# An earlier opening, a feed-forward convolution tracked by halves, and paired output stores in an eight-core decoder-block kernel

## The chip, the cores and the metric

One Trainium2 chip (trn2), eight cores, one launch of one program on all of them. The metric is the device time of the slowest core, in microseconds (us). The eight cores sit on two dies (cores 0 to 3 and 4 to 7). In some executions the cores of one die or of both run at a lower granted TensorE clock and the time is some per cent longer; such runs are called slow here and are left out of every comparison. The engines are PE (matmul), PEld (its weight load), DVE (vector), ACT (scalar, with lookup tables), POOL (GpSimd) and SP (SyncE); POOL and SP issue the DMAs.

## The reference

A decoder block for a batch of 4 sequences of 2048 tokens with 2048 features, all float32:

```python
h = rmsnorm(x)
b, c, u, q, k, v, o, i, f = split(h @ w_in)
y_c = b * dwconv3_causal(c * u)                  # short gated convolution, 1024 channels
y_m = sigmoid(o) * rmsnorm_per_head(mlstm(q, k, v, i, f))   # 4 heads, a recurrence over the sequence
x = x + concat(y_c, y_m) @ w_out
g, u = split(dwconv3_causal(rmsnorm(x) @ w_up) + bias)      # 2 x 5632 channels
x = x + (silu(g) * u) @ w_down
x = x + sigmoid(rmsnorm(x) @ w_ple_gate) * (p @ w_ple_proj)
out = rmsnorm_final(x)
```

Each sequence is shared by two cores. The even core ("role 0") owns the first 1056 tokens, the odd core ("role 1") the last 992; because of the recurrence, role 1 also reads the tokens before its own, in slabs of 128, and computes their keys and gates.

## The kernel before

One program holds the instruction lists of both roles. Each engine reads its role from memory and branches:

```python
def both(e, eng):
    v = eng.value_load(role)
    with eng.If(v == 0):
        run(progs[0], e, eng)
    with eng.Else():
        run(progs[1], e, eng)
```

The lists come from Python code. `P.op` and `mm` append an instruction at once; `later(instruction, priority, waits)` puts it into a pool from which a scheduling model picks by modelled readiness and priority (0 first), `need(item)` forces it out, `flush_items()` empties the pool at the end. So the order on each engine is fixed at build time, and an engine executes its list in order: an instruction that waits holds up all that stand behind it.

The opening of role 1 (cuts marked `...`):

```python
P.op("sp", ... cst <- cst_p)                 # constants
if role:
    slab_load(0)
    slab_load(1)
P.op("sp", ... tct <- cst_t)                 # tables
P.op("pool", ... wif <- w_if)                # gate weights
P.op("pool", ... ident_bf <- cst_i)          # identity
...
def prefix_k(pump):                          # role 1
    k0, k1 = ip["k0"], ip["k1"]              # the first two key weights, 4 loads each
    slab_load(2, [k0.loads[2]])              # waits for a weight load
    pump()
    slab_load(3, [k1.loads[2]])
    ...
```

The feed-forward convolution. The up projection comes in units `c`; the first few handle one slice of the tokens at a time (there are two slices), the others both. Behind each unit stands this chain on ACT and DVE, and the units behind it need ACT for the copies that free PSUM:

```python
HW = NOWN // 2                               # where the two halves of the buffer are cut
RYv = [[RS("yv%d%d" % (j, h), Yo[j] + 4 * HW * h, 4 * HW) for h in range(2)] for j in range(2)]
...
def f():
    a = 0 if 0 in slices else 2 * QE - OFF   # where the two slices meet
    e_ = NOWN if 1 in slices else 2 * QE - OFF
    ...
    prev = cmult.get("last", [])             # the last product, of whatever slice
    yh = [h for h in range(2) if h * HW < e_ and h * HW + HW > a]
    for j in range(2):                       # gate half, value half
        it = later(s_act(yv, C(OFF), AF.Identity, ... bias, scale=w[2]), 1, ev + prev)    # ACT
        for t in (1, 0):
            it = later(s_stt(yv[:, z:], C(OFF - 2 + t + z)..., w[t], ...), 1, [it])       # DVE
        if j == 0:
            it = later(s_act(yv, yv, AF.Silu, Ry, Ry), 1, [it])                           # ACT
        fin.append(it)
    ...
    ms.append(later(s_tt(... ALU.mult ...), 1, fin))                                      # DVE product
    cmult["last"] = ms
```

The end: after the last gate unit of a slice, 16 normalisation products and 16 stores:

```python
def final(s):
    def f():
        nf.rs(s)
        for k in range(16):
            x, Rx = nf.xs(k, s)
            i = later(s_stt(x, x, cs(PC_GF + k), nf.acc[s], ...), 1, nf.rdy[s])
            later(("sp", ... outTv[:, k, 2*QO*s : 2*QO*(s+1)] <- x ...), 1, [i])
    return f
...
run_units(units, slots)
flush_items()
```

The softmax here doesn't subtract the row's maximum and nothing guards it: scores larger than these inputs give would overflow.

## Time and profile before

| | before |
|---|---|
| time, median of the first 5 runs | 1611.38 us (1611.2 to 1839.99, the highest a slow run) |
| span of the profiled run, even cores | 1596.9 to 1601.0 us |
| span of the profiled run, odd cores | 1605.0 to 1609.1 us |
| PE busy | 92% of the span |

A line of a timeline reads: start in us, busy us, engine, line of the program, operation, output<-input, count, and in brackets how long the engine had stood idle before and what released it. Nearly every instruction passes through a helper, so the line numbers mostly name the helper: in the kernel before, 328 is ACT, 333 and 337 are DVE, 352 is a matmul; in the changed kernel these are 334, 339, 343 and 358. Lines 348 (before) and 354 (changed) are transposes, lines from 1000 on DMAs and memsets of the opening. A line of a windows view gives the busy time of each engine in a stretch and, as its last three numbers, the granted clock, the DMA share and GB/s. An ACT_TABLE_LOAD marks a change of function on ACT; as every run has the same sequence of them, they serve as milestones.

### The profile page before, as it was taken

The page shows a single profiled execution, that of the slowest core. Times are in us where ns is not written, and L with a number is a line of the kernel's source. Part 1 is how long each engine was busy: PE and PEld are TensorE (multiplying, and loading weights), DVE is VectorE, ACT ScalarE, POOL GpSimd, SP SyncE. Part 2 cuts the span into 40 slices and gives each one's busy share as a digit, 9 for nine tenths or more (in the row PEclk, how much of TensorE's full clock was granted, in tenths as well). Part 3 has the DMA queues.
Part 4 walks back from the last instruction along what each step waited for, and adds up shares of the span by engine and source line. Part 5 has one row for each costly group of instructions (what it writes and reads, how often), then busy time and mean ns, then how long its engine had stood idle before and what let it go on. Part 6 is the DMA issues. An engine that isn't in the chain of part 4 may idle for free.

```text
span 1609.1 us, 36850 instructions; the slowest of 8 cores (1596.9 to 1609.1 us)
## 1 busy us (share of the span) xinstructions
PE 1485.8 (92%) x13634; PEld 1267.8 (79%) x13634; DVE 1169.8 (73%) x1802; ACT 592.8 (37%) x1054; POOL 248.4 (15%) x472
## 2 busy tenths in 40 slices
PE   2989999999998997999999999999999998998984
PEld 2865899898877885888888888888898886866763
DVE  2464333387768787888788877888778887879976
ACT  1652324577421123443034420444302444223453
POOL 1001111011112010111211122111121112211100
PEclk9989999999999998999999999999999999999997
DMA  6901644445758242464666556555566665745413
GB/s 166 318 31 26 101 85 74 96 62 123 152 81 149 35 73 47 67 92 61 84 107 91 78 71 104 91 89 80 79 89 98 91 88 86 99 68 85 78 66 138
DMA packets 80937, 148.82 MB, mean 92 GB/s; under 512 B 9072, under 2 KB 34288, under 8 KB 79728
## 3 DMA queue, kind: packets, MB, share of 16 engines
q0 software_dynamic: 67648, 112.90, 46.5%
q1 hardware_dynamic: 13104, 33.47, 6.0%
q8 instruction: 114, 1.87, 0.5%
q14 instruction: 71, 0.58, 0.1%
HBM read 251.08 MB, written 8.13 MB: 161 GB/s over the span
## 4 chain that ended last, share of the span: by engine, by line
PE 78%; DMA 8%; DVE 6%; issue 4%; ACT 2%; SPq 1%; POOL 1%; DVEq 0%; POOLq 0%; ACTq 0%
PE PS L352 77%; DVE M L333 3%; DMA M<-w_down_p 3%; DVE M L337 3%; ACT M L328 2%; DMA M<-xsl 1%; DMA M<-xr 1%; DMA M<-w_in_p 1%; DMA M<-pT 1%; PE PS L348 1%; DMA M<-w_up_p 1%; POOL M L588 0%; DMA M<-w_pg_p 0%; ACT L328 0%; SPq L1018 0%
## 5 line engine op out<-in xcount | busy, mean ns | idle before, releaser
L352 PE MATMUL PS<-M 128*128 128x250 bf16 (+6 forms) x13330 | 1473.3, 270 | 105.1 <-ACT M L328 42.9
L352 PEld LDWEIGHTS PS<-M 128*128 128x128 bf16 (+1 forms) x13330 | 1249.7, 99 | 320.4 <-issue 166.2
L333 DVE TENSOR_TENSOR M<-M 128x992 bf16<-128x992 f32 (+18 forms) x716 | 494.9, 710 | 86.6 <-PE PS L352 40.7
L328 ACT ACTIVATE M<-PS 128x500 f32<-128x500 f32 (+8 forms) x490 | 238.2, 494 | 542.5 <-PE PS L352 532.8
L337 DVE SCALAR_TENSOR_TENSOR M<-M 128x992 f32<-128x992 f32 (+9 forms) x378 | 353.5, 981 | 54.3 <-ACT M L328 52.9
L328 ACT ACTIVATE M<-M 128x992 f32<-128x992 f32 (+10 forms) x398 | 308.6, 803 | 220.4 <-DVE M L333 154.9
L333 DVE TENSOR_TENSOR M<-M,PS 128x496 f32<-128x496 f32 (+6 forms) x443 | 251.1, 568 | 115.2 <-PE PS L352 110.7
L333 DVE TENSOR_TENSOR M<-PS,M 128x500 f32<-128x500 f32 (+13 forms) x191 | 102.0, 538 | 128.5 <-PE PS L352 115.4
L588 POOL DMA_DIRECT2D M<-w_up_p x176 | 93.1, 529 | 473.3 <-DVE M L333 228.8
L588 POOL DMA_DIRECT2D M<-w_in_p x96 | 50.9, 535 | 392.3 <-PE PS L352 211.7
L328 ACT ACTIVATE PS<-PS 128x500 f32<-128x500 f32 (+1 forms) x57 | 31.3, 549 | 214.1 <-PE PS L352 214.0
L588 POOL DMA_DIRECT2D M<-w_down_p x128 | 67.7, 529 | 229.1 <-PE PS L352 173.6
L328 ACT ACTIVATE M<-PS,M 126x256 bf16<-126x256 bf16 (+4 forms) x68 | 30.1, 483 | 15.5 <-DVE M L333 12.7
L588 POOL DMA_DIRECT2D M<-w_pg_p x32 | 16.9, 532 | 96.0 <-PE PS L352 89.7
L588 POOL DMA_DIRECT2D M<-w_out_p x32 | 16.9, 531 | 57.4 <-PE PS L352 52.3
L1156 DVE COPY M<-PS 128x1024 bf16<-128x1024 bf16 x9 | 6.2, 691 | 25.2 <-PE PS L348 25.2
L348 PE MATMUL PS<-M 128*128 128x128 bf16 (+4 forms) x304 | 22.6, 219 | 1.3 <-ACT M L328 0.9
L348 PEld LDWEIGHTS PS<-M 128*128 128x128 bf16 (+4 forms) x304 | 19.9, 110 | 3.1 <-issue 2.6
L328 ACT ACT_TABLE_LOAD x9 | 11.5, 1283 | 9.6 <-DVE M L1025 7.0
L337 DVE SCALAR_TENSOR_TENSOR M<-M,PS 128x256 f32<-128x256 f32 x24 | 10.7, 476 | 0.0
L1027 DVE CAST M<-M 128x128 bf16<-128x128 f32 x1 | 0.4, 365 | 13.6 <-DMA M<-cst_i 13.6
L328 ACT ACTIVATION_READ_ACCUMULATOR M<-PS 126x1 f32 (+1 forms) x32 | 6.4, 200 | 0.0
(22 smaller groups left out, 12.4 us busy)
## 6 DMA issues: line engine op xcount, KB each, us to landing
M<-w_up_p POOLq DMA_DIRECT2D x176, 256.0 KB, 4.8
M<-w_in_p POOLq DMA_DIRECT2D x96, 256.0 KB, 6.1
M<-w_down_p POOLq DMA_DIRECT2D x64, 192.0 KB, 4.2
M<-w_down_p POOLq DMA_DIRECT2D x64, 160.0 KB, 3.9
M<-xsl SPq DMA_DIRECT2D x8, 1024.0 KB, 10.6
M<-w_out_p POOLq DMA_DIRECT2D x32, 256.0 KB, 5.9
M<-w_pg_p POOLq DMA_DIRECT2D x32, 256.0 KB, 5.5
M<-xr SPq DMA_DIRECT2D x32, 250.0 KB, 7.6
```

Source lines behind the costliest of these rows:

```text
L328: return ("act", lambda e: e.activation(out=out, in_=in_, func=func, **kw), reads, writes, c)
L333: return ("dve", lambda e: e.tensor_tensor(out=out, in0=in0, in1=in1, op=op), reads, writes, c)
L337: return ("dve", lambda e: e.scalar_tensor_tensor(out=out, in0=in0, scalar=scalar, in1=in1, op0=op0, op1=op1), reads, writes, c)
L348: return ("pe", lambda e: e.transpose(out, in_, ident), reads, writes, 0.065)
L352: return ("pe", lambda e: e.matmul(out, lhsT=lhsT, rhs=rhs, start=start, stop=stop, skip_group_check=skip), reads, writes, c)
L588: p.loads.append(P.op("pool", lambda e, d=d, sr=sr: e.dma_start(out=d, in_=sr), [], [p.R[nm]], dma=True, cost=p.KT * 0.25, after=g))
L1027: P.op("dve", lambda e: e.tensor_copy(out=ones_bf, in_=onesF), [Rcst], [Rcbf])
L1156: it = later(("dve", lambda e, o=tr_out, i=tr_in: e.tensor_copy(out=o, in_=i), [RPS[7]], tr_R, 1.2), 0)
```

## The change

Its intent is to take idle time of PE out of three places: the opening (start the big loads before the role is known, and let the longer role fall through the branch), the first units of the up projection (let the convolution of one slice not wait for the other's product), and the end (fewer and larger stores, final products out of the way). A fourth part turns the ring of weight slots round, so that the first key weights have the same address in both roles. The core of the diff:

```diff
+COMMON = {"sp": 2, "pool": 5}
 ...
         def both(e, eng):
+            n = COMMON.get(e, 0)
+            run(progs[0], e, eng, 0, n)          # constants, xf; identity, 4 loads of k0
             v = eng.value_load(role)
-            with eng.If(v == 0):
-                run(progs[0], e, eng)
+            with eng.If(v == 1):
+                run(progs[1], e, eng, n)
             with eng.Else():
-                run(progs[1], e, eng)
+                run(progs[0], e, eng, n)
 ...
+    xf_op = P.op("sp", ... 1.08 MB block: slab 1 in role 1, feature tiles 0 to 3 in role 0)
 ...
     def prefix_k(pump):
         k0, k1 = ip["k0"], ip["k1"]
-        slab_load(2, [k0.loads[2]])
+        wif_load()
+        slab_load(2)
         pump()
         slab_load(3, [k1.loads[2]])
-        for c in range(4, NSB + 1):
+        for c in range(4, NSB + 2):
             slab_load(c)
 ...
-    ring = [Slot(GB + 2048 * i, 0, 10 ** 9) for i in range(NRING)]
+    ring = [Slot(CB - 2048 * (i + 1), 0, 10 ** 9) for i in range(NRING)]
+    ip["k0"].pin = dict(zip(RAWQ, ring))
 ...
-    HW = NOWN // 2
+    HW = 2 * QE - OFF
 ...
+    clast = [[], []]
 ...
-            prev = cmult.get("last", [])
-            yh = [h for h in range(2) if h * HW < e_ and h * HW + HW > a]
+            prev = [it for h in slices for it in clast[h]]
+            yh = slices
 ...
-            cread[c] = rd                        # the steps that read unit c's buffers
+            cread.setdefault(c, []).extend(rd)   # ... of both slices
 ...
-            cmult["last"] = ms
+            for h in slices:
+                clast[h] = ms
 ...
-                i = later(s_stt(x, x, cs(PC_GF + k), ...), 1, nf.rdy[s])
-                later(("sp", ... one tile ...), 1, [i])
+                its.append(later(s_stt(x, x, cs(PC_GF + k + j), ...), 2, nf.rdy[s]))
+            later(("sp", ... two tiles ...), 2, its)
 ...
     run_units(units, slots)
+    fill(10.0 ** 9, 0.0)                         # emit leftover work by modelled readiness
     flush_items()
```

Cut are the data preparation for `xf`, the new order and conditions of the other opening loads, a rewriting of the last stage's code for a mode that is not used (`if False`), and the memsets that moved earlier.

## The prediction

> **What bounds the kernel now.** I read the spans of all cores first. The program has two roles: even cores own 1056 tokens of a sequence (role 0), odd cores own 992 and in addition work through the prefix of their sequence (role 1). The time is that of the slowest core.
>
> ```profile
> core 0: 1596.9 us, clock 0.982
> core 1: 1609.1 us, clock 0.977
> core 4: 1601.0 us, clock 0.980
> core 5: 1605.0 us, clock 0.979
> ```
>
> The reader is to see that the odd cores set the time (1605.0 to 1609.1) and that the even ones follow 4 to 12 us behind (1596.9 to 1601.0). So a gain in role 1 counts only down to what role 0 then takes. PE is busy 92% on both, in steady stages 99 of 100 us; a change that leaves the matmuls alone can win only in the stages where PE idles. I looked for these with 100 us windows on cores 0 and 1: PE is busy 61 to 62 us in the first hundred, 86 to 87 in the one that holds the start of the up projection, 87 to 91 in 1300 to 1500, and idle in the last 17 to 20 us. These are the stages that the diff touches.
>
> The opening: SyncE's queue in the timeline of core 0, then core 1, then core 1's chain of waits.
>
> ```profile
> 2.51 0.39 SPq L1018 DMA_DIRECT2D M<-cst_p  x1
> 2.95 0.42 SPq L1022 DMA_DIRECT2D M<-cst_t  x1
> ...
> 6.52 4.60 SPq L1018 DMA_DIRECT2D M<-cst_p  x1
> 11.18 0.89 SPq L1011 DMA_DIRECT2D M<-xsl  x2
> ...
> 26.14 12.31 SPq L1011 DMA_DIRECT2D M<-xsl  x7
> ...
> 2.38 4.14 issue
> 6.52 4.60 SPq L1018
> 11.65 7.56 DMA M<-xsl
> 20.78 13.50 DMA M<-w_in_p
> 36.83 15.67 DMA M<-xsl
> ```
>
> Role 0 starts its first DMA at 2.51 us. Role 1, which sits in the Else half, starts it at 6.52 and the second one 4.6 us later. Nothing in the program lies between; both gaps are 4.0 and 4.2 us. Then slab 1, the first key weights and slab 2 arrive in turn, and PE does its first real matmul at 27.44 us and reaches the steady part at 37.7.
>
> The up projection (core 1, then core 0), the last up unit (core 1), and the end (core 1's last DVE group; core 0's windows, whose last three numbers are clock, DMA share and GB/s):
>
> ```profile
> 639.65 1.50 ACT L328 ACTIVATE M<-M 128x500 f32<-128x500 f32 x2 [2.61 <-DVE M L333]
> 641.77 3.49 PE L352 MATMUL PS<-M 128*128 128x250 bf16 x16 [8.25 <-ACT PS L328]
> ...
> 572.32 3.02 PE L352 MATMUL PS<-M 128*128 128x264 bf16 x13 [7.21 <-ACT PS L328]
> ...
> 1363.65 0.37 PE L352 MATMUL PS<-M 128*128 128x248 bf16 x1 [6.45 <-DVE M L333]
> ...
> 1594.93 10.43 DVE L337 SCALAR_TENSOR_TENSOR M<-M 128x496 f32<-128x496 f32 x16 [4.61 <-ACT M L328]
> ...
> 1591.00:1592.00 1.00, 0.00 (x0) 0.00 (x0) 0.00 (x0) 0.00 (x0) 0.00 (x0) 0.50 0.48 182
> 1596.00:1597.00 1.00, 0.00 (x0) 0.00 (x0) 0.00 (x0) 0.00 (x0) 0.00 (x0) 0.50 0.00 0
> ```
>
> PE waits 8.25 and 7.21 us for a PSUM copy on ACT, which stands behind a chain of convolution steps that alternate between ACT and DVE. At the end core 0's outputs have landed by 1592, yet its span goes on to 1596.9; core 1's DMA ends near 1607.4 and its span at 1609.1.
>
> **What the Trainium skill says.** "Runtime: NRT & Kernel Launch", section "Instruction fetch mechanics": prefetch is sequential, and a taken branch to a target outside the current two pages must fetch that page first. The trace agrees: role 1 jumps at the start (first DMA 4.0 us later than role 0), role 0 jumps over the other body at the end (about 4 us without data traffic). "DMA: Bandwidth & Descriptors", section "Anatomy of one DMA — SWDGE (gpsimd) path": about 2.0 us fixed plus bytes over 436 GB/s. The lone output DMAs of 248 KB landed in 2.1 us here, below that sum of 2.6; in the opening the engines are saturated (share 1.0) at 310 to 350 GB/s for plain loads, and I use these. "ScalarE: Activation LUTs", section "What ACT_TABLE_LOAD costs": 1283 ns; the trace has 1.28 us for each load, one of them inside the convolution chain.
>
> **The change, part by part.**
>
> Part 1, the opening. Constants, a 1.08 MB block "xf" (slab 1 in role 1; the first 4 of 16 feature tiles in role 0), the identity and the 4 first weight loads go ahead of the role's register load and branch; the branch is turned round, so role 1 falls through and role 0 jumps.
> Role 1: first DMA at about 1.0 instead of 6.5, slab 1 issued at about 1.4 instead of 11.6. Weights k0 (1 MB as bf16, 2 MB read) issued at about 2 to 4 instead of 13 to 15. Bytes read before k1 has landed: 0.3 constants, 1.1 slab 1, 2 k0, 0.1 and 0.2 tables, 0.2 slab 0, 1.05 slab 2 (it no longer waits for k0), 2 k1: 6.9 MB, at 310 GB/s 22 us, plus 2: the second weight pair is there at about 24 to 25. Before, the steady part began at 37.7, so 12 to 13 us are gained. After that PE has 9 to 10 of 10 us busy until 80, so it keeps the gain if the loads keep up: slabs 3 to 8 and the first half of its own tokens are 10.4 MB, at 330 GB/s 32 us from 23, so landed by 57; PE wants them from about 62. I take 12.
> Role 0: the jump moves to its front. SyncE would issue tile 4 at about 11 instead of 5.8. But by then 3.4 MB have been issued, which keep the DMA engines busy to about 13, so there is no hole; the other 12 tiles and gate weights (3.5 MB, 11 us) are in by about 25, as now (chain: last xr wait ends at 24.5). I take 0, plus or minus 3.
> At the end the jump changes sides as well: role 0 saves about 4 us (its 4.9 us after the outputs, less the 1.6 that core 1 needs, is 3.3 to 4), role 1 pays 4.
>
> Part 2, the convolution by halves. Sliced units used to wait for the previous product whatever its half, and in role 1 the halves of the buffer were cut at 496 although the slices meet at 492, so slice 1 really waited for both. Now each half has its own list and cut. DVE's idle gaps in that chain are 2.21 + 1.05 + 1.50 + 1.00 = 5.8 us on core 1 and 1.79 + 1.08 + 1.56 + 0.94 = 5.4 on core 0; two independent chains can fill most of them, but DVE has 14 us of convolution to do there in any case, and the kernel's own scheduling model decides the order. I take 4 us in role 1 and 3 in role 0. At the last up unit role 1 loses its wait on the product (1.04 us): 1.
>
> Part 3, the end. Outputs leave as 8 pairs of tiles instead of 16 tiles per slice, normalisation products have the lowest priority, and leftover work is emitted by modelled readiness. The last product group is 16 instructions by 0.65 us, 10.43 us, unchanged; its DMA is now twice as large, at most 0.6 us more. The first slice's products stand in DVE's way in the last 40 us (PE waits 0.5 to 1.7 us each, about 5 in all on core 1): 1 us gained net.
>
> Part 4, the ring of weight slots is turned round and k0 pinned in it; same number of slots. 0.
>
> Sums: role 1: 1609.1 - 12 - 4 - 1 - 1 + 4 = 1595; role 0: 1601.0 + 0 - 3 - 1 - 4 = 1593 at most, core 0 near 1589. The slowest is then a role 1 core at 1595, and the measured time stands 2.3 us above the span (1611.38 against 1609.1): **1597 us**, 0.9% less.
>
> **The rivals.** (a) The opening of role 1 is bound by total DMA traffic, not by its start: its engines are at share 1.0 from 15 to 80 us. Then the gain is the earlier start of real traffic, 12 to about 3, with some idle time given back: 8 to 9 instead of 12, and the time 1601. For it: the chain names xr loads until 74.6. Against: PE and ACT did not wait for them there. (b) Role 0 becomes the bound: its jump costs 4 us twice (first and second page, as role 1 shows) and a hole in DMA appears, so its first norm slips by 5 or more. Then core 4 stands at 1598 and the time at 1600 to 1602. For it: POOL in role 1 had its first DMA as late as 11.80. Against: the common block covers that time. (c) Part 2 works fully and the modelled order suits: 8 us instead of 4 in each role, and the time is 1592. (d) The new order of products and pairs costs at the end, where little overlaps: up to 3 us, 1600.
>
> **Range and chances.** The rivals lie from 1592 to 1602, and cores of one role differ by 4 us in one run: low 1589, high 1605. Over 2% faster would need less than 1579: all of PE's idle time in the opening and the up stage together; 4%. Slower by over 2% has no mechanism, except a new serial wait that I have not seen: 1%. Within 2%: 95%.
>
> **What would show it.** In the changed kernel: first DMA of every core near 1 us; role 1's slab 1 landed by 10, its steady key matmuls from about 25, and everything in it about 12 us earlier at 200 us; role 0 with its second group of DMAs near 6 to 11 us and its first norm still ending near 33; PE's 8.25 and 7.21 us waits in the up stage halved; about 4 us between last output and end on odd cores, under 2 on even ones. I am wrong if role 1 at 200 us is less than 8 us ahead, if even cores become the slowest by more than 3 us, or if the up stage keeps its waits.

## The result, and the profile after

| | before | changed |
|---|---|---|
| time, median | 1611.38 us (15 runs, 1608.39 to 1839.99) | 1587.15 us (8 runs, 1586.15 to 1588.92) |
| ratio of the fast runs | | 0.9851, 95% interval 0.9841 to 0.9861 |
| profiled run, even cores | 1596.9 to 1601.0 us | 1579.9 to 1582.1 us |
| profiled run, odd cores | 1605.0 to 1609.1 us | 1580.9 to 1583.5 us |

A ratio is the mean time of one kernel's fast runs over that of the other's fast runs of the same rounds, so it is not quite the ratio of the medians in the table. The change is worth 1.5%: within 2%, as predicted, but 24 us rather than 14, and 1587.15 us lies below the predicted range of 1589 to 1605.

The cores of the changed kernel:

```profile
core 0: 1580.3 us, clock 0.988
core 1: 1581.5 us, clock 0.981
core 3: 1583.5 us, clock 0.983
```

The two roles, 8 us apart before, now end nearly together. The milestones on one core of each role show where the time went (start of the instruction in us; the difference is how far ahead the changed kernel is, and a step between rows is what a stage gave):

| milestone | core 1 before | after | ahead | core 0 before | after | ahead |
|---|---|---|---|---|---|---|
| 2nd table load, opening is over | 192.00 | 178.77 | 13.2 | 110.27 | 115.18 | -4.9 |
| 3rd table load | 317.16 | 303.92 | 13.2 | 235.85 | 240.76 | -4.9 |
| silu table load, up projection starts | 630.22 | 617.13 | 13.1 | 563.18 | 565.27 | -2.1 |
| third PSUM copy of the full up units | 670.41 | 644.32 | 26.1 | 601.09 | 591.86 | 9.2 |
| table load at the end of the up stage | 1428.91 | 1402.42 | 26.5 | 1397.40 | 1390.00 | 7.4 |
| start of the last slice | 1559.30 | 1533.47 | 25.8 | 1541.32 | 1531.56 | 9.8 |
| last table load | 1592.24 | 1561.60 | 30.6 | 1575.36 | 1562.11 | 13.3 |
| end | 1609.1 | 1581.5 | 27.6 | 1596.9 | 1580.3 | 16.6 |

Three places give the time: the opening (role 1 only; role 0 loses there), the 40 us after the silu table load (13 and 11 us), and the last slice (4.8 and 3.5 us). The last row has the branch and the new stores at the end: role 1 gives back 3.0, role 0 gains 3.3. The other steps of core 0 (2.8 us before the silu table load, 2.4 us before the last slice) are stretches that vary by as much between cores; they come under what stays open.

The opening after, first core 1, then core 0, from their timelines:

```profile
1.07 0.39 SPq L1049 DMA_DIRECT2D M<-cst_p  x1
3.21 0.07 DVE L1060 MEMSET M<- 128x9 f32 x1 [3.21 <-issue]
7.51 0.33 SPq L1051 DMA_DIRECT2D M<-cst_t  x1
...
19.72 10.11 PE L358 MATMUL PS<-M 128*128 128x8 bf16 x136 [0.57 <-DMA M<-w_if]
...
29.67 0.61 PE L354 MATMUL PS<-M 128*128 128x128 bf16 x8
```

```profile
1.06 0.39 SPq L1049 DMA_DIRECT2D M<-cst_p  x1
10.92 0.06 DVE L1060 MEMSET M<- 128x1 f32 x1 [10.92 <-issue]
15.55 0.33 SPq L1051 DMA_DIRECT2D M<-cst_t  x1
```

and the line of before, core 1, that answers to the last one of the first fence:

```profile
43.48 0.61 PE L348 MATMUL PS<-M 128*128 128x128 bf16 x8
```

Both cores start their first DMA at 1.06 to 1.07 us. The transposes that come with the second key weights stand 13.8 us earlier on core 1. The jump is now role 0's: DVE, which has nothing to wait for, starts at 10.92 us where core 1's starts at 3.21, and SyncE resumes only at 15.55 us (12.9 to 15.6 on the four even cores), after what looks like a second stop, as role 1 had it before between 6.52 and 11.18 us.

The up projection of before, core 1, timeline (the two lines that stand after the second of these, at 639.65 and 641.77, are in the prediction):

```profile
630.22 1.28 ACT L328 ACT_TABLE_LOAD   x1
...
638.82 0.74 DVE L333 TENSOR_TENSOR M<-M 128x248 bf16<-128x248 f32 x2
...
641.06 0.57 ACT L328 ACTIVATE PS<-PS 128x500 f32<-128x500 f32 x1
```

and after, core 1:

```profile
607.46 0.79 ACT L334 ACTIVATE M<-M 128x500 f32<-128x500 f32 x1
...
609.19 0.79 ACT L334 ACTIVATE M<-M 128x500 f32<-128x500 f32 x1
...
617.13 1.28 ACT L334 ACT_TABLE_LOAD   x1
618.43 0.61 ACT L334 ACTIVATE M<-M 128x492 f32<-128x492 f32 x1
618.95 0.57 ACT L334 ACTIVATE PS<-PS 128x500 f32<-128x500 f32 x1
619.45 0.60 ACT L334 ACTIVATE M<-M 128x500 f32<-128x500 f32 x1
...
623.51 26.73 PE L358 MATMUL PS<-M 128*128 128x250 bf16 x246 [1.31 <-ACT M L334]
```

The copy that PE waits for is the ACTIVATE from PS to PS. Before, it starts 10.8 us after the silu table load. In front of it on ACT stand the first convolution steps of slice 1 of the first unit (639.65, the gate's and the value's), and they wait for DVE's product of slice 0 (638.82). The program puts them there: before a full unit `c` is emitted, `up_unit` forces out (`need`) the steps that read the buffers of unit `c - 2`, and with one list slice 1's steps draw the whole chain of slice 0, over two units, out with them. Now these steps wait for no product and have run at 607.46 and 609.19, before the table load; the copy starts 1.8 us after it, and what stands behind it (619.45) is, by its place in the chain, the silu of slice 1. PE's wait of 8.25 us is gone; 1.31 us are left.

The windows of core 0, one line and the sum of the stretch, first before (556 to 606 us), then after (556 to 596 us):

```profile
566.00:576.00 10.00, 3.68 (x16) 2.26 (x16) 6.84 (x12) 4.12 (x6) 0.30 (x1) 0.66 0.17 26
...
sum 50.00, PE 39.07 PEld 31.97 DVE 40.79 ACT 23.49 POOL 7.15; mean PE 7.81 PEld 6.39 DVE 8.16 ACT 4.70 POOL 1.43
```

```profile
566.00:576.00 10.00, 9.95 (x88) 8.24 (x86) 9.11 (x16) 7.50 (x12) 2.12 (x4) 1.00 0.54 82
...
sum 40.00, PE 38.59 PEld 32.39 DVE 36.65 ACT 22.63 POOL 6.96; mean PE 9.65 PEld 8.10 DVE 9.16 ACT 5.66 POOL 1.74
```

The same ten microseconds, before and after: before, 16 matmuls took 3.68 us at a granted clock of 0.66; after, 88 matmuls took 9.95 us at 1.00. PE's idle time in the stretch falls from 10.9 to 1.4 us (50.00 - 39.07 and 40.00 - 38.59). DVE's falls too, from 9.2 to 3.4 us.

The end, core 1's last product group from its timeline, then its windows:

```profile
1564.29 10.43 DVE L343 SCALAR_TENSOR_TENSOR M<-M 128x496 f32<-128x496 f32 x16 [4.20 <-ACT M L334]
```

```profile
1577.00:1578.00 1.00, 0.00 (x0) 0.00 (x0) 0.00 (x0) 0.00 (x0) 0.00 (x0) 0.50 0.69 226
1578.00:1579.00 1.00, 0.00 (x0) 0.00 (x0) 0.00 (x0) 0.00 (x0) 0.00 (x0) 0.50 0.11 38
1579.00:1580.00 1.00, 0.00 (x0) 0.00 (x0) 0.00 (x0) 0.00 (x0) 0.00 (x0) 0.50 0.08 22
```

The products take the same 10.43 us as before. Most of the output is out by about 1577.7 us, but some traffic goes on until 1580: the last store was issued at 1574.87 and took 5.4 us to land (3.0 before), so it is in at 1580.3. The span goes on to 1581.5. From the last product to the end it is 6.8 us, against 3.8 before.

### The profile page after: what moved, and what is told of

Read it like the earlier page. It is cut to its first block, busy times and chain, and to the rows that moved or that the text cites. A ratio compares the mean times of both kernels' runs of the same rounds, so it can differ in the third digit from the quotient of the medians.

```text
span 1583.5 us, 36809 instructions; the slowest of 8 cores (1579.9 to 1583.5 us)
## 1 busy us (share of the span) xinstructions
PE 1477.0 (93%) x13634; PEld 1263.7 (80%) x13634; DVE 1167.1 (74%) x1802; ACT 592.3 (37%) x1054; POOL 248.5 (16%) x472
## 4 chain that ended last, share of the span: by engine, by line
PE 82%; DVE 5%; DMA 5%; issue 4%; ACT 2%; POOL 0%; SPq 0%; POOLq 0%; DVEq 0%; ACTq 0%
PE PS L358 82%; DVE M L339 3%; DVE M L343 2%; DMA M<-xr 2%; ACT M L334 2%; DMA M<-w_down_p 2%; DMA M<-w_in_p 1%; PE PS L354 1%; POOL M L597 0%; DMA M<-w_up_p 0%; ACT L334 0%; SPq L1042 0%; POOLq L220 0%; DVEq L210 0%; ACT PS L334 0%
## 5 line engine op out<-in xcount | busy, mean ns | idle before, releaser
L334 ACT ACTIVATE M<-PS,M 126x256 bf16<-126x256 bf16 (+4 forms) x68 | 30.1, 482 | 15.5 <-DVE M L339 12.8
(22 smaller groups left out, 12.6 us busy)
```

The source lines that it names most:

```text
L334: return ("act", lambda e: e.activation(out=out, in_=in_, func=func, **kw), reads, writes, c)
```

## The experiments

Twelve kernels ran, in three groups; each group ran on one chip together with the kernel before. The changed kernel did not run again in these groups: its row is from the first comparison. Since the roles behave differently, the clearest measure is the mean span of each role over its four cores and over all fast runs:

| kernel | even cores | odd cores | ratio to before, 95% interval |
|---|---|---|---|
| before (in the three groups) | 1598.1 to 1598.8 | 1607.6 to 1608.2 | |
| changed | 1581.2 | 1583.1 | 0.9851 (0.9841 to 0.9861) |
| changed without part 2 | 1596.5 | 1592.9 | 0.9929 (0.9908 to 0.9951) |
| changed, one list | 1595.3 | 1591.7 | 0.9913 (0.9897 to 0.993) |
| changed, old cut | 1580.1 | 1584.5 | 0.984 (0.982 to 0.986) |
| before with part 2 | 1584.8 | 1595.5 | 0.9922 (0.9905 to 0.994) |
| changed, branch turned back | 1584.6 | 1582.9 | 0.986 (0.9842 to 0.9877) |
| changed, no common loads | 1587.2 | 1581.3 | 0.9872 (0.9853 to 0.9891) |
| changed, role read first | 1581.2 | 1584.6 | 0.9853 (0.9834 to 0.9872) |
| changed, role first, gates late | 1582.1 | 1585.8 | 0.9862 (0.984 to 0.9884) |
| changed, two common blocks | 1580.3 | 1588.1 | 0.9869 (0.9849 to 0.9888) |
| changed, old priority | 1582.5 | 1585.4 | 0.9865 (0.9847 to 0.9882) |
| changed, no emission at the end | 1585.5 | 1584.3 | 0.9857 (0.984 to 0.9873) |
| changed, single stores | 1581.6 | 1583.8 | 0.9846 (0.9826 to 0.9865) |

The slowest core sets the time and the roles are now 2 us apart, so a microsecond lost in one role shows in the time only partly. Differences of about 1 us in this table are not to be trusted: the changed kernel with one list differs by 1.2 us from the one without part 2 on even cores too, where the programs differ in nothing that the role uses. All results were correct.

### Part 2: the convolution by halves

The theory: the single list, through the order on ACT, held PE's copy behind the other slice's product, and its removal is what the prediction undervalued. First part 2 was undone alone, list and cut:

```diff
-            prev = [it for h in slices for it in clast[h]]
+            prev = cmult.get("last", [])
...
-            cread.setdefault(c, []).extend(rd)
+            cread[c] = rd
...
-            for h in slices:
-                clast[h] = ms
+            cmult["last"] = ms
-    HW = 2 * QE - OFF
+    HW = NOWN // 2
```

> The changed kernel with part 2 (convolution by halves) taken back, all else kept. Theory A, that part 2 was the mis-sized term and is worth 12 to 14 us in each role by itself: the PSUM copy of the first full up unit waits again behind the convolution chain, PE waits 7 to 8 us there, and the time is about 1600 us. Rival B, that part 2 is worth the 4 us predicted and the rest of the gain between 560 and 640 us comes from the other parts through a changed emission order: about 1591 us and a PE wait of at most 3 us there.

Measured: 1599.9 us, 12.8 more than the changed kernel. Even cores lose 15.3 us and odd ones 9.8. From the third table load to the third PSUM copy core 0 needs 364.8 us (351.1 changed, 365.2 before) and core 1 349.2 (340.4 and 353.3). From the silu table load to the first of these copies it is 8.4 us again on every even core and 10.8 on every odd one, as in the kernel before.

Then part 2 alone, put into the kernel before (the same lines, the other way):

> The kernel before with part 2 alone. Theory A: both roles lose 12 to 14 us between the end of the mixer and the second full up unit, the slowest core goes from 1609 to about 1596 and the time to 1598 us. Rival B: 4 us, 1607 us.

Half of its runs were slow, and the median of 1646 us is therefore useless; the three fast ones lie at 1597.24 to 1599.5 us, ratio 0.9922. The profiled run was slow on the first die; on the undisturbed one the same stretch takes 351.3 us on core 4 (366.9 before) and 340.0 on core 5 (350.7 before). The mean span falls by 13.6 us on even cores and 12.6 on odd ones. So part 2 gives 9.8 to 15.3 us in each role with the rest of the change or without it.

Which of its two edits carries it? The list undone, the cut kept (the `cread` line, which belongs to the two lists, went back with it and was not tried by itself):

```diff
-            prev = [it for h in slices for it in clast[h]]
+            prev = cmult.get("last", [])
...
-            cread.setdefault(c, []).extend(rd)
+            cread[c] = rd
...
-            for h in slices:
-                clast[h] = ms
+            cmult["last"] = ms
```

> The changed kernel, but the products of the convolution wait again for the last product of whatever half (one list), while the halves keep the new cut. Theory A (the list alone is what let PE's wait go; the cut adds little): both roles fall back to the numbers of the run without the whole of part 2, third table load to the third PSUM copy of the up stage 362 to 366 us on core 0 (351.1 changed, 364.8 without part 2) and 347 to 350 on core 1 (340.4 and 349.2), time near 1600. Theory B (in role 1 the cut carries half of it): core 0 near 364, but core 1 in the middle, 343 to 346, because a chain that waits for the right half only is already the gain there; time still near 1598, then set by role 0.

Measured: 1598.78 us; 364.7 us on core 0 and 349.3 on core 1. Theory A holds: both are within 0.1 us of the run without the whole of part 2. The timeline of core 0 has the stall back:

```profile
575.16 3.52 PE L358 MATMUL PS<-M 128*128 128x264 bf16 x16 [7.21 <-ACT PS L334]
```

It is the 7.21 us wait of the kernel before, to the hundredth, and the 16 matmuls behind it run at half speed again (3.52 us for 16, against 9.95 for 88 above).

The cut alone undone:

```diff
-    HW = 2 * QE - OFF
+    HW = NOWN // 2
```

> The changed kernel with its two lists, but the buffers cut in the middle of the tokens again (496 in role 1, where slices meet at 492; in role 0 both are 528, so nothing changes there). Theory A (the list carries it): role 1 loses at most 1 us, stretch from the third table load to the third PSUM copy 340 to 342 on core 1, time 1587 to 1588. Theory B (slice 1 of role 1 overlaps both halves of the buffer and so truly waits for the other slice's product): the old stall comes back in role 1 alone, 345 to 349 us on core 1 and 351 on core 0, time 1592 to 1596 with the odd cores slowest. Also: the wait of PE before the last up unit on core 1 (6.45 before, 5.65 changed) goes back to about 6.4 under B.

The profiled run was slow on the first die, so cores 4 and 5 are read: 350.9 and 341.2 us (350.8 and 338.5 in the changed kernel). The fast runs have the ratio 0.984, no worse than the changed kernel. Theory A's time holds, and B's 345 to 349 us does not come. What the cut does can be seen at the last up unit, in the timelines of core 5, first with the old cut, then in the changed kernel:

```profile
1341.26 0.37 PE L358 MATMUL PS<-M 128*128 128x248 bf16 x1 [6.45 <-DVE M L339]
```

```profile
1337.10 0.37 PE L358 MATMUL PS<-M 128*128 128x248 bf16 x1 [5.65 <-DVE M L339]
```

With the old cut the wait is the 6.45 us of the kernel before, with the new one it is 0.8 us shorter. On this point B was right: slice 1 does wait for the other half. But it is worth 0.8 us there and about 1 us in the first units (core 7; core 5's 2.7 us may include the 2 us by which that stretch varies between odd cores), and nothing that the time shows.

### Part 1: the opening

Does turning the branch round pay? Undone alone:

```diff
-            with eng.If(v == 1):
-                run(progs[1], e, eng, n)
+            with eng.If(v == 0):
+                run(progs[0], e, eng, n)
             with eng.Else():
-                run(progs[0], e, eng, n)
+                run(progs[1], e, eng, n)
```

> The changed kernel with the order of the two bodies as before (role 0 falls through, role 1 jumps at the start), common loads kept. Theory A, that a jump taken while the DMA engines are full costs 8 to 9 us instead of 4 (role 0 in the changed kernel: first DVE instruction at 10.9 us against 3.2 on role 1): role 1 has its first DVE instruction near 11 us and its SyncE again near 15, its steady part starts 4 to 6 us later (34 to 36 instead of 29.7), it ends 3 us sooner behind its last output; role 0 starts its first norm 5 to 7 us earlier (32 to 33 instead of 38.5) and ends 3 us later. Slowest core is role 1 by about 2 us more than now: 1589 us. Rival B, that the jump costs about 4 us at either end and only moves between roles: unchanged, 1587 us. Rival C, that the start-up of role 1 is bound by DMA traffic alone: role 1 gains the 3 us at its end and the time falls to 1584.

The time came out as expected, 1589.7 us, but by another path than theory A's, so this is luck: the slowest core was an even one. Role 1's transposes start at 32.8 us (29.67 changed), less of a loss than expected. Role 0's first normalised block starts at 35.78 us (38.45 changed, 33.74 before): even when it falls through, role 0 is 2 us later than before, so not all of its loss is the jump. At the end role 0 pays: 23.3 us from the last table load against 18.2, and role 1 takes 17.2 against 19.9. On balance the branch gives even cores 3.4 us and odd ones nothing (0.2). One thing goes against theory A and stays unexplained: SyncE of role 1, which jumps here, resumes at 7.5 to 7.8 us on the four odd cores, earlier than that of role 0, which falls through (8.5 to 9.9); the stop until about 15 us did not come. DVE of role 1 does pay (first instruction at 9.5 to 10.5 us, against 3.1 to 5.6 in role 0).

The common loads undone, with the branch turned as in the changed kernel:

```diff
-COMMON = {"sp": 2, "pool": 5}
+COMMON = {}
```

> The changed kernel with nothing ahead of the branch (role 1 still falls through). Theory A: most of role 1's 13 us come from falling through, since with loads in flight the role read and the fetch that follow cost SyncE 5.6 us instead of 1.4. Then role 1 has its first DMA near 2.5 us and its first transposes between 28 and 32 (29.7 now); role 0 has its first DMA near 6.5, its second near 11 and its first norm at 42 to 43 (38.5 now); time 1588 to 1590 with role 0 the slowest. Rival B, the early loads are what gave role 1 its gain: its first transposes at 34 or later and the time 1591 or more, with role 1 the slowest.

Measured: 1591.7 us. Core 1's transposes start at 29.55 us, as with the common loads. So once role 1 falls through, the early loads are worth nothing to it. (Undone singly, the branch and the loads leave its transposes at 32.80 and 29.55 us, against 43.48 before; a run with both undone, which would show what the reordered loads are worth by themselves, was not made.) The early loads matter to role 0, whose SyncE then looks like this (core 0, timeline):

```profile
6.79 4.31 SPq L1049 DMA_DIRECT2D M<-cst_p  x1
11.15 0.42 SPq L1050 DMA_DIRECT2D M<-xf  x1
...
42.09 3.48 DVE L343 SCALAR_TENSOR_TENSOR M<-M 128x528 bf16<-128x528 f32 x5 [26.65 <-ACT M L334]
```

That is role 1's start of before, 6.79 for 6.52 and 11.15 for 11.18: whichever role jumps has it, where no common loads stand ahead of the branch. The first normalised block slips from 38.45 to 42.09 us and the even cores lose 6.0 us (the odd ones end 1.8 earlier). The hoisted block is what makes the turned branch bearable for role 0.

In the changed kernel SyncE of role 1, which only falls through, resumes as late as 7.51 us. The suspect was the read of the role behind the loads already issued. So the role was read first:

```diff
-            run(progs[0], e, eng, 0, n)
             v = eng.value_load(role)
+            run(progs[0], e, eng, 0, n)
```

> The changed kernel with the role read ahead of the common loads instead of behind them (the branch stays behind them). Theory A, the 5.6 us between the common loads and the rest in role 1 are the read of the role behind full DMA queues: SyncE of role 1 resumes at 3.5 to 5 us instead of 7.5, slab 0 lands before 13 instead of 17.8, PE's first matmul at 14 to 16 instead of 18.6, first transposes near 27 instead of 29.7; role 0, whose jump still fetches under load, resumes near 14 to 16 as now. Time 1585 to 1587. Rival B, it is the instruction fetch: SyncE resumes at 7 or later and all is 1.4 us later: 1588.5.

SyncE of core 1 then resumes at 3.35 us, so the suspicion was right; but the transposes come at 33.52 us, where about 27 was expected, because PE waits 6.50 us for the gate weights. Time 1587.6 us, no gain. A larger common block was tried the same way, two slabs or eight feature tiles instead of one slab or four tiles:

```diff
-COMMON = {"sp": 2, "pool": 5}
+COMMON = {"sp": 3, "pool": 5}
...
-    "xf": dt_in("xf", [128, XF])
+    "xf": dt_in("xf", [128, 2 * XF])      # and slab 2 / tiles 4 to 7 taken from it
```

> The changed kernel with a second common block of 1.08 MB ahead of the branch: tiles 4 to 7 in role 0, slab 2 in role 1. Theory A: role 0's first norm (38.5 us now, 33.7 in the kernel before) is late because its DMA engines run dry at 14 to 20 us (share 0.41 to 0.75) while SyncE is away for the jump, and because the key weights now stand ahead of its tiles: with 8 tiles ahead it comes at 34 to 36. Role 1 is nearly unchanged, first transposes 29 to 31. Time 1585 to 1587, since role 1 is then the slowest. Rival B, role 0's first norm is bound by total traffic: it stays at 37 or later.

Role 0's first normalised block starts at 36.14 us, between the two theories, and its cores end 0.9 us earlier, no more than the noise. But role 1's transposes slip to 36.53 us, where 29 to 31 was expected, and its cores lose 5.0 us: time 1591.3 us.

The last try joined the early role read with an order in which PE does not need the gate weights first:

```diff
             v = eng.value_load(role)             # before the common loads, as above
...
+            if c >= NSP:
+                gates_(c)
+        def gates_(c):
             for k in range(16):
                 mm(PS[...], hTp[:, c, k, 0:P_], wif[:, k, 0:8], ...)
...
         for c in range(NSP):
             first(c)
             keys(c, [0])
+        for c in range(NSP):
+            gates_(c)
```

> A try at a better version: the changed kernel, but the role is read before the common loads (an earlier run showed SyncE of role 1 free at 3.35 instead of 7.51 us, but PE then stood 6.5 us for the gate weights), and the products with the gate weights for the first three slabs stand behind the three first key products. Theory A (PE's wait for the gate weights was what took the gain away): no such wait of more than 1 us, first transposes of role 1 at 26 to 28.5 us (29.67 changed, 33.52 with the early role read alone), time 1584 to 1586, then bound by role 0. Theory B (the opening of role 1 is bound by the bytes ahead of the second key weights): the wait only moves to another weight, first transposes at 29.5 to 34, time 1587 to 1589.

Theory B holds. On core 1 PE's wait has moved to another weight (timeline), and the transposes start at 33.76 us; the time is 1589.0 us:

```profile
23.12 10.80 PE L358 MATMUL PS<-M 128*128 128x256 bf16 x136 [6.61 <-DMA M<-w_in_p]
```

Every attempt to start role 1 sooner ends in a wait for some transfer. No version tried beats the changed kernel by more than the width of the intervals.

### Part 3: the end

The products' priority alone undone:

```diff
-                                       Rx + [nf.Racc[s], Rcst], Rx), 2, nf.rdy[s]))
+                                       Rx + [nf.Racc[s], Rcst], Rx), 1, nf.rdy[s]))
...
-            later(("sp", ... two tiles ..., Rk, [], 0.003 * n), 2, its)
+            later(("sp", ... two tiles ..., Rk, [], 0.003 * n), 1, its)
```

> The changed kernel with the final normalisation products and their stores at the old priority 1, pairs kept. Theory A, that low priority is what made the last slice of the last stage 4 to 5 us shorter in role 1 and 3 to 4 us in role 0: the last table load comes that much later and the time is about 1591 us. Rival B, that emission by readiness at the very end did it: at most 1 us, 1588 us.

1589.2 us, between the theories (and by its interval, 0.9847 to 0.9882, not resolved from the changed kernel). The last slice, between the last two table loads, takes 31.2 us on odd cores (28.1 changed, 32.9 before) and 31.5 on even ones (30.5 changed, 34.0 to 34.5 before). The priority is thus 3.0 of 4.8 us in role 1, but only about 1 of 3.5 to 4 in role 0. For the rest the emission before the flush was removed:

```diff
     run_units(units, slots)
-    fill(10.0 ** 9, 0.0)
     flush_items()
```

> The changed kernel without the emission of leftover work by modelled readiness before the rest is flushed. The last slice (between the last two table loads) took 28.1 us on core 1 and 30.6 on core 0 changed, 32.9 and 34.0 before, and 31.2 and 31.5 with the priority of the products undone. Theory A (this emission carries the part that the priority leaves, 1.8 us in role 1 and 2.6 in role 0): the slice takes 30 us on core 1 and 33 on core 0, time 1589 to 1590. Theory B (the low priority carries it, and this emission acts only after the last unit): the slice unchanged within 0.7 us, and only the time from the last table load to the end moves, by up to 2 us; time 1586 to 1589.

The last slice takes 29.8 us on odd cores and 33.5 on even ones: theory A, and with the priority's part the sums close (3.0 + 1.7 of 4.8, and 0.9 + 3.0 of about 3.7). Even cores end 4.3 us later. The time, 1589.12 us with a ratio of 0.9857, is not resolved from the changed kernel's 0.9851; the slices are.

Stores of single tiles again:

```diff
-            later(("sp", ... outTv[:, k:k + 2, o:o + n] <- xx ..., Rk, [], 0.003 * n), 2, its)
+                later(("sp", ... outTv[:, k + j, o:o + n] <- x ..., Rx, [], 0.75), 2, [its[-1]])
```

> The changed kernel with 16 stores of single tiles per slice instead of 8 of pairs. Theory A, pairs lengthen the end, because the first store waits for two products and the last one is twice as large (from the last table load to the end role 0 took 23.3 us with role 0 falling through and pairs, against 21.5 in the kernel before): from the last table load to the end 1 to 2 us less in role 0 and 0.5 to 1 in role 1, time about 1586. Rival B, the end is set by the 16 products and the jump: within 0.4 us, 1587.

1587.7 us, ratio 0.9846; from the last table load to the end 18.6 us on core 0 and 21.1 on core 1 (18.2 and 19.9 changed). The rival theory's time holds, and theory A has the wrong sign: on all four odd cores singles take longer from the last table load to the end (21.1 to 21.8 us, against 19.7 to 20.1 changed), on the even ones slightly (18.6 to 18.9 against 18.2 to 18.3). In the mean spans this is 0.7 and 0.4 us, less than can be trusted. In this run the second table load on core 1 came at 183.2 us, with an unchanged opening; in the changed kernel's profile the four odd cores lie at 178.8 to 182.2. Role 1's opening varies by a few microseconds between cores and launches.

## Why the prediction was right or wrong

**The verdict and the bottleneck were right.** The time stayed within 2%. Rival (b), that role 0 becomes the bound, came true in its means (the jump, the hole in role 0's DMA) but not in its end: over the fast runs the slowest odd core stands at 1585.4 us on average and the slowest even one at 1582.6.

**Part 1, role 1: right.** Predicted 12 us, measured 13.2 on core 1, and 11 by the medians of the odd cores (191.3 to 180.3 us at the second table load). Its reason was partly wrong. The prediction put the gain down to loads issued at 1.4 us, but without the common loads role 1 is as fast; and with role 1 jumping again it keeps all but 3.1 of the 13.8 us at its transposes. How much the reordered loads give by themselves stays open. Rival (a), that bytes bind this opening, did not lower the gain, but fits that each later try ended in a wait for a transfer.

**Part 1, role 0: wrong, "I take 0, plus or minus 3".** Core 0 lost 4.7 us at its first normalised block, the even cores 3.6 at the second table load (medians 110.7 and 114.3). The failed step is "SyncE would issue tile 4 at about 11": it did so after 15.55 us. So "there is no hole" failed as well: in the windows of core 0 changed the DMA share falls to 0.41 at 16 to 18 us and 0.75 at 18 to 20. The jump cost DVE 7.7 us (10.92 against 3.21; 7.3 to 8.3 over the four pairs of cores), not the 4.0 that the start of role 1 showed before. Without the common loads the same jump of role 0 costs DVE 4.2 us (6.82 against 2.63 on core 1 of that run), so on DVE the loads already issued are what makes it longer. For SyncE this is not settled: with the branch turned back, role 1 jumps under the same loads and its SyncE resumes no later than the other role's. The turned-back branch shows that about 2 us of the loss are not the jump; that those come from the key weights ahead of role 0's tiles is argued, not shown.

**Part 2: the wait was the right one, but what bounds the gain was wrong, and this is the main error: 4 and 3 us predicted.** The runs show 9.8 to 12.6 us in role 1 and 13.6 to 15.3 in role 0. The failed step is "DVE's idle gaps in that chain are ... 5.8 us on core 1 ... and 5.4 on core 0". It took DVE as the resource that bounds the gain. PE, however, did not need DVE's work; it needed one ACT copy whose data were ready, and that copy stood in ACT's list behind an instruction waiting for the other slice. With two lists that instruction runs before the copy comes. Nearly all of PE's wait went (8.25 to 1.31 us on core 1), and DVE's work was done beside PE's. The list changes both the order on ACT and the wait at run time; the runs do not separate the two. The windows size it on core 0: the stretch is 10 us shorter and holds 343 matmuls instead of 332, 11 more at 0.1125 us, so 11.2 us in all. Of these 9.5 are PE's idle time (10.9 less 1.4), and 1.7 are matmuls that no longer run slowly (39.07 us for 332 against 38.59 for 343, or 0.0052 us each). On core 1 the same reckoning over 622 to 672 and 609 to 649 us gives 8.4 us of idle time and 3.7 of slow matmuls. The second term was missing from the prediction altogether, though a page describes it: the Trainium skill, "TensorE: Matmul & The Clock Gate", section "What's actually happening", says that PE falls to half its clock after about 3.4 us of idleness and needs about 3.4 us of work to come back. After the 7.21 us wait a 264-column matmul took 0.22 us (3.52 / 16, in the run with one list), elsewhere 0.1125, and after the remaining wait of 1.31 us on core 1 the granted clock was 1.00.

Rival (c) had the right direction with "8 us instead of 4 in each role", and was still too small. At the last up unit 1 us was predicted and 0.8 came.

**Part 3: "1 us gained net" was too small.** The last slice gave 4.8 us in role 1 and about 3.7 in role 0. The prediction saw the priority (3.0 and 0.9 us) but gave the emission by modelled readiness nothing; it is worth 1.7 and 3.0. The pairs of stores, for which up to 0.6 us was charged, cost nothing that shows; at the end of role 1 the profile has them faster by 1.0 to 2.1 us than singles. Rival (d) is refuted.

**The branch at the end: the net was right, the reading behind it was not.** From the last table load to the end role 0 saves 3.3 us (4 predicted) and role 1 pays 3.0 (4 predicted). But the prediction took core 0's outputs of before to have landed by 1592; the last one was issued at 1589.45 and took 4.3 us, so it was in at 1593.7, and 3.1 us were left, not 4.9. On core 1 changed, about 4 us were forecast between the last output and the end, and 1.3 came; the rest of what role 1 pays is the longer landing of its last store. That landing changes with both the branch and the pairs, so these 3.0 us are not the jump alone.

**The sum.** With the measured terms on core 1, 1609.1 - 13.2 - 13.0 - 4.8 + 3.0 is 1581.1, and its span is 1581.5. Against the prediction's terms the up stage gave 9 us more and the end 4; the range was built from rivals of 1592 to 1602, each failing alone, and had no room for two terms failing in the same direction.

**What stays open.** Two stretches take one of two lengths without a cause that a run shows: from the third table load to the silu one 311 or 313 us on odd cores of the changed kernel and 325.6 or 327.3 on even cores of the kernel before; and on even cores of the changed kernel the stretch before the last slice 105.9 or 108.4 us. They blur the exact worth of part 2 in role 1 by about 2 us. Why the leftover work, emitted by readiness, gains more in role 0 than in role 1 was not followed further. And part 4, the ring of weight slots, was not undone by itself.

## What to carry to other kernels

When an engine waits for an instruction, look at what stands before that instruction in its own in-order list. If its data are long there, the wait is worth all that PE loses, slow matmuls after it included, and not the idle time of whatever engine appears as the last releaser. A dependency that is wider than the data needs it to be (one list for two halves) costs most where it makes an in-order engine stand still in front of work for someone else. And where two roles share a program, every cost that is moved from one to the other should be measured under the load that will then be there: the jump that cost DVE about 4 us with empty queues cost it nearly 8 behind 3 MB of loads.

## What the Trainium skill lacked or had wrong

- "Runtime: NRT & Kernel Launch", section "Instruction fetch mechanics", says that a taken branch out of the current pages stalls, but gives no size. Here it was 4.0 us on SyncE with nothing in the DMA queues (first DMA at 6.52 against 2.51 us; 3.0 to 4.0 over the four odd cores) and 7.7 us on DVE with about 3 MB queued (10.92 against 3.21 us); right after it, SyncE stood over 4 us more between two DMA issues (6.52 to 11.18 us before), which fits a second fetch but is not shown to be one.
- The same section gives about 0.2 us for reading a register from memory. Behind the loads of the common block SyncE of role 1 was held from the issue of the block at 1.51 us until 7.51; with the read ahead of them it was free at 3.35 us. That an engine's read can be held so long behind loads that it issued itself stands there nowhere. (DVE, which had issued none, was past its read by 3.21 us in the same execution.)
- "DMA: Bandwidth & Descriptors", section "Anatomy of one DMA — SWDGE (gpsimd) path": 2.0 us plus bytes over 436 GB/s gives 2.6 us for 248 KB. The page gives this sum for POOL's path alone; the lone output stores of the kernel before, issued by SyncE, landed in 2.1 us, so it does not carry over to them.
- No page has a way to bound what removing a wait on an in-order engine is worth. Here the gaps on the releasing engine suggested 5 to 6 us, and the runs gave 10 to 15.
